# Down projection of a feed-forward block as seven block products in place of eight, in four parts shifted by one tile

## Chip, cores and metric

The kernel runs on one core of one Trainium2 chip. The metric is the device time of one execution in microseconds (us), the median of several runs. Five engines work side by side, each on its own queue in order: TensorE (PE; its weight loads are shown as PEld), VectorE (DVE), ScalarE (ACT), GpSimd (POOL), and SyncE (SP), which issues DMAs. POOL issues the accumulating DMAs.

## What is computed

One layer of a streaming encoder over 512 prompt tokens and 64 sample tokens (576 columns in all), model width 1024: a mixer with two linear-attention branches, a cross attention into 256 memory tokens, a feed-forward with a short convolution, and a last norm. The change lies in the feed-forward:

```python
def _conv_ffn(h, w_up, conv_w, conv_b, w_down, prev):
    u, new = _causal_dwconv(h @ w_up, conv_w, prev)      # width 3, along the tokens
    u = u + conv_b
    gate, val = u[..., :D_FF], u[..., D_FF:]             # D_FF = 2816 = 22 blocks of 128
    return (jax.nn.silu(gate) * val) @ w_down, new
...
x = x + f.astype(x.dtype)
...
y = _rmsnorm(x, p['norm_final'])
```

All of it is in fp32.

## The kernel before

**Layout.** Activations lie transposed: features on the 128 partitions, the 576 tokens along the free axis. A weight tile is 128 output features by up to eight blocks of 128 input features. An fp32 product is three matmuls on rounded operands (fp32r): each operand is split into a high part and a rest, and high x high, high x rest (activation's rest) and rest x high (weight's rest) are summed in PSUM. Names: `xh`/`xl` and `ach`/`acl` are high and rest of activations, `wh`/`wl` of weights, `wr` the raw weight from HBM.

**Weights.** `emit_weight` loads a raw tile (three raw buffers, `RAWB`), and for up and down projection makes the rest in three steps: ACT writes minus the raw weight, rounded, into `wl`; ACT casts the raw weight into `wh`; an accumulating DMA, issued by POOL, adds the raw weight to `wl`. For other weights, VectorE or POOL subtracts (`X` takes the one that the planner expects to be done first). `weight` hands out a tile and prepares one tile ahead (`LA`).

**Order.** The order on every engine is written by a planner in the kernel (`Driver`): TensorE's matmuls are taken in program order, and each instruction of another engine is put where the planner's own costs say that its engine is free, at most 6 us (`BACK`) before TensorE's planned time. Side work runs in generators (`spawn`) which go on when their inputs are planned to be ready. The chip then runs each queue in that order; semaphores do the rest.

**Feed-forward.** Two halves of 11 blocks. In each half, for each block, `tile_proj("up", ...)` runs the gate tile and the value tile (8 blocks x 3 terms x 2 column ranges = 48 matmuls each), and `up_finish` takes them out of PSUM with the norm's factor (`fu`), runs the three-step convolution (`fc`, one scaled copy and two multiply-adds on VectorE), then SiLU on ACT, the product of gate and value, and the split into `ach` and `acl`. Then the down projection of that half: for each of the eight output tiles, the 11 blocks go into one two-bank PSUM tile (`big`), in column ranges of 256 and 322 (two columns of padding between prompt and sample included), and VectorE adds the result to `x[m]`. With `late=True`, all matmuls with `wh` stand ahead of those with `wl`.

**End.** In the second half, each finished `x[m]` is squared (`sq`), summed (`acc`) and scaled with the last norm's gain (`gx`). The last output tile, 7, is computed in two column ranges (`half`), so that the norm and the transposes of the first (`c_out`, `rtf`, `yo`) run beside the matmuls of the second. PSUM has two `big` tiles and four single banks (`sm`).

Of the kernel before, what the change touches and what calls it, by code (L numbers as in the profile page):

```python
# [22 lines left out]
KT = D // P  # L23
EPS = 1e-6
NJ = 22
FH = 11
SLOT = 584
LA = 1
NS = 57
RAWB = 3  # L30
WB = 3
NGDN = 2
HOP = 0.2
BACK = 6.0
# [9 lines left out]
C_CB = 224  # L44
# [17 lines left out]
def weight_order():  # L62
    seq = list(HEADS)
    for m in range(8):
        seq += [("gta", m), ("gtb", m)]
    seq += [("out", m) for m in range(8)]
    seq += [("wo", m) for m in range(8)]
    for hd in range(4):
        seq += [("mk", 2 * hd), ("mk", 2 * hd + 1)]
        if hd % 2 == 0:  # L70
            seq += [("mv", 2 * hd + i) for i in range(4)]
        seq += [("mq", 2 * hd), ("mq", 2 * hd + 1)]
    seq += [("mo", m) for m in range(8)]
    for f in range(2):
        for j in range(FH * f, FH * f + FH):
            seq += [("up", j), ("up", NJ + j)]
        for m in range(8):
            seq += [("dn", (m, f, 0)), ("dn", (m, f, 1))]
    return seq


WORDER = weight_order()
WFULL = [w for w in WORDER if w[0] != "dn"]
WIDX = {w: i for i, w in enumerate(WFULL)}
NW = len(WFULL)

# [4 lines left out]
WAIT = "wait"  # L91
# [267 lines left out]
def tile_trunk(ctx, tc, xT, memT, wt, wd, vec, cst, w0, wgate, st_gdn, st_conv, st_gla, st_ffn, ckT, cv,  # L359
# [30 lines left out]
    def big():  # L390
        return drv.rotate("big", 2, pb.tile([P, 2, 512], F32, tag="big", name=nm("big")))
# [7 lines left out]
    def f(ap):  # L399
        return ap.bitcast(F32)  # L400
# [2 lines left out]
    wpos = [0]  # L403
    wready = {}

    def emit_weight(i):
        kind, idx = WORDER[i]
        raw = drv.rotate("raw", RAWB, wp.tile([P, 1024], F32, tag="raw", name=nm("wr"), bufs=RAWB))
        if kind == "dn":
            m, fh, part = idx  # L410
            n = (6 if part == 0 else 5) * 128
            c0 = fh * FH * 128 + part * 768
            DMA(raw[:, :n], wd[m, :, c0:c0 + n])
        else:
            n = 1024
            DMA(raw, wt[WIDX[(kind, idx)]])
        h = drv.rotate("wh", WB, wp.tile([P, 1024], F32R, tag="wh", name=nm("wh"), bufs=WB))
        lo = drv.rotate("wl", WB, wp.tile([P, 1024], F32R, tag="wl", name=nm("wl"), bufs=WB))
        if kind in SUMMED:
            A.activation(lo[:, :n], raw[:, :n], AF.Copy, scale=-1.0)  # L420
            A.copy(h[:, :n], raw[:, :n])
            drv.accumulate(lo[:, :n], raw[:, :n], nc.gpsimd)
# [5 lines left out]
    def weight(kind, idx, ahead=LA):  # L428
        i = wpos[0]
        assert WORDER[i] == (kind, idx), (WORDER[i], kind, idx)  # L430
        wpos[0] = i + 1
        for j in range(i, min(i + ahead + 1, len(WORDER))):
            if j not in wready:
                emit_weight(j)
        return wready[i]


    ones_r = cp.tile([P, 128], F32R, name="onesr")
# [30 lines left out]
    def vcol(c, n=1):  # L469
        return vec_t[:, c:c + n]  # L470
# [53 lines left out]
    def two(t_, o1=0, o2=TP):  # L524
        return r4(t_[:, o1:o1 + TP], 256), t_[:, o2:o2 + TS]
# [692 lines left out]
    def main():  # L1218
        acc = slot("acc")
        xg = []  # L1220
        for i in range(2):
            wready[i] = tuple(wp.tile([P, 1024], F32R, tag=t_, name=nm(t_), bufs=WB) for t_ in ("wh", "wl"))
            drv.rotate("wh", WB, wready[i][0])
            drv.rotate("wl", WB, wready[i][1])
        acc2 = slot("acc")
        s1 = slot("sq")

# [244 lines left out]

        drv.spawn(c_rstat("n3", [(acc, 0)], 4, True, 2.0))
        CW = 578

        def up_finish(col, ps):
# [5 lines left out]
            G.tensor_copy(fout[:, col, 2:4], u[:, 578:580])  # L1482
            c = slot("fc")
# [6 lines left out]
        for fh in range(2):  # L1490
            act = []
            for j in range(FH * fh, FH * fh + FH):
# [6 lines left out]
                c0 = up_finish(j, ba_[0])  # L1499
                A.activation(c0[:, 0:CW], c0[:, 0:CW], AF.Silu)  # L1500
                if j > 0:
                    yield from tile_proj("up", NJ + j, xs, bb_)
                c1 = up_finish(NJ + j, bb_[0])
                X.tensor_tensor(c0[:, 0:CW], c0[:, 0:CW], c1[:, 0:CW], op=ALU.mult)
                h, lo = slot("ach", F32R), slot("acl", F32R)
                A.copy(h[:, 0:CW], c0[:, 0:CW])
                X.tensor_tensor(lo[:, 0:CW], c0[:, 0:CW], f(h[:, 0:CW]), op=ALU.subtract)
                act.append((h[:, 0:CW], lo[:, 0:CW]))
            if fh == 0:
                for m in range(8):  # L1510
                    ps = big()
                    wh, wl = weight("dn", (m, fh, 0))
                    yield from proj(ps, wh, wl, act[0:6], True, False, CW, late=True)
                    wh, wl = weight("dn", (m, fh, 1))
                    yield from proj(ps, wh, wl, act[6:11], False, True, CW, late=True)
                    xx = two(x[m])
                    V.tensor_tensor(xx[0], xx[0], ps[:, :, 0:256], op=ALU.add)
                    V.tensor_tensor(xx[1], xx[1], ps[:, 1, 258:322], op=ALU.add)
            else:
                DMO(o_ffn, fout)  # L1520

        acc = slot("acc")
        gx = []
        for m in range(7):
            ps = big()
            wh, wl = weight("dn", (m, 1, 0))
            yield from proj(ps, wh, wl, act[0:6], True, False, CW, late=True)
            wh, wl = weight("dn", (m, 1, 1))
            yield from proj(ps, wh, wl, act[6:11], False, True, CW, late=True)
            xx = two(x[m])  # L1530
            V.tensor_tensor(xx[0], xx[0], ps[:, :, 0:256], op=ALU.add)
            V.tensor_tensor(xx[1], xx[1], ps[:, 1, 258:322], op=ALU.add)
            sq_acc(acc, x[m], m == 0)
            g = slot("gx")
            A.activation(g[:, 0:T], x[m][:, 0:T], AF.Identity, scale=vcol(C_GFIN + m))
            gx.append(g)
        m = 7
        wa, wb = weight("dn", (m, 1, 0)), weight("dn", (m, 1, 1))
        sq7, g7 = slot("sq"), slot("gx")
        gx.append(g7)  # L1540

# [42 lines left out]
                    yield 0.0  # L1584

        def half(o, c):
            k = 0
            for (wh, wl), n in ((wa, 6), (wb, 5)):
                for i in range(n):
                    mm3([(o, c)], wh, wl, act[k][0], act[k][1], i, k == 0, k == 10)  # L1590
                    k += 1
                    yield 1.0

        halves = [sm(), big()[:, 0, :]]
        yield from half(halves[0][:, 0:322], slice(256, CW))
        last_evac(halves[0], (256, TP, 0), (TP, T, 258))
# [51 lines left out]
def pack_inputs(inp):  # L1648
# [26 lines left out]
    wd = np.stack([kp(a["w_down"][0][:, P * m:P * m + P]) for m in range(8)])  # L1675

    w0 = np.zeros((D, 32), np.float32)
    w0[:, 0:16] = w_in[:, off["glr"]:off["glr"] + 16]
# [62 lines left out]
```

## Time and profile before

| | |
|---|---|
| median of 3 runs | 1157.0 us (1156.87 to 1157.26) |
| the profiled execution | 1155.68 us, span of its instructions 1153.8 us |
| TensorE busy | 1131.2 us (98%), granted clock 0.996 on average |
| VectorE, ACT, POOL busy | 639.0 (55%), 476.3 (41%), 287.3 us (25%) |
| moved by DMA | 133.66 MB, 116 GB/s on average |

Busy time of TensorE is a modelled figure, since matmuls overlap; the chain of waits and the distance between the starts of matmuls say more. The program's lines nearly all show as one helper line (L179 before), so tiles' names tell the instructions apart: `big<-xh,wh` is an up projection (and others ahead of it), `big<-ach,wh` a down projection, `x<-x,big` its addition to the residual, `wl<-wr` on ACT the negation and on POOL the issue of the accumulating DMA. In groups of instructions the figures are count | busy us, mean ns of one | idle time of the engine ahead of them and what ended it.

### The profile page before, as it was taken

Reading aid. Unit: us, or ns where it says so; the run is one execution under the profiler, and the core shown is the slowest. Engines: PE = TensorE matmul, PEld = TensorE weight load, DVE = VectorE, ACT = ScalarE, POOL = GpSimd, SP = SyncE. Lnnn points to the kernel's source line nnn. Section 1 sums busy time; section 2 is a strip of 40 time slices with the busy share of each in tenths; the row PEclk is TensorE's granted clock in tenths of the full one; section 3 lists DMA queues with packets and bytes.
Section 4 is the critical chain, followed back from the end, with each engine's and each line's share of the span. In section 5 each row is a group of like instructions: output and inputs, shape, how many; then the busy total and the mean of one; then the engine's idle time right before and its main releaser. Section 6 shows DMA issues by size and latency. Waiting matters only on the chain.

```text
span 1153.8 us, 20892 instructions
## 1 busy us (share of the span) xinstructions
PE 1131.2 (98%) x8573; PEld 1092.4 (95%) x8573; DVE 639.0 (55%) x1122; ACT 476.3 (41%) x900; POOL 287.3 (25%) x470
## 2 busy tenths in 40 slices
PE   8989999999999999999999999999999999999998
PEld 7889899989889999999999999999999999999998
DVE  7798557687454347656565554566561036566213
ACT  5445336335443243234444343533433333443443
POOL 4473127533112011002021100322221122222211
PEclk9999999999999999999999999999999999999999
DMA  6131101211213233434334314577667877677773
GB/s 233 37 91 41 47 15 57 77 39 42 70 31 128 76 110 102 143 97 135 110 124 141 129 55 109 131 167 175 169 139 171 170 174 173 162 163 156 163 165 116
DMA packets 46862, 133.66 MB, mean 116 GB/s; under 512 B 5424, under 2 KB 10800, under 8 KB 46768
## 3 DMA queue, kind: packets, MB, share of 16 engines
q1 hardware_dynamic: 35824, 97.74, 26.8%
q0 software_dynamic: 10944, 34.61, 16.9%
q8 instruction: 67, 1.10, 0.4%
q14 instruction: 27, 0.22, 0.1%
HBM read 92.35 MB, written 5.37 MB: 85 GB/s over the span
## 4 chain that ended last, share of the span: by engine, by line
PE 89%; DVE 7%; ACT 1%; issue 1%; DMA 1%; SPq 0%; POOL 0%; ACTq 0%; DVEq 0%
PE big L179 76%; PE sm L179 13%; DVE c L179 3%; DMA x<-xT 1%; DVE acc L179 0%; DVE xl L179 0%; SPq L179 0%; ACT c L179 0%; DVE u L179 0%; DVE gc L179 0%; DVE tg L179 0%; DVE z L179 0%; DMA wr<-wt 0%; DVE gy L179 0%; ACT th L179 0%
## 5 line engine op out<-in xcount | busy, mean ns | idle before, releaser
L179 PE MATMUL big<-xh,wh 128*128 128x256 f32 (+1 forms) x1536 | 339.1, 302 | 2.6 <-DVE sg L179 1.8
L179 PE MATMUL big<-xl,wh 128*128 128x256 f32 (+1 forms) x1536 | 328.5, 295 | 1.8 <-DVE xl L179 1.8
L179 PE MATMUL big<-xh,wl 128*128 128x256 f32 (+1 forms) x1536 | 280.1, 296 | 1.5 <-DVE wl L179 1.3
L179 PEld LDWEIGHTS big<-xh,wh 128*128 128x128 f32 x1536 | 254.0, 189 | 7.4 <-issue 2.1
L179 PEld LDWEIGHTS big<-xl,wh 128*128 128x128 f32 x1536 | 258.1, 189 | 2.7 <-DVE xl L179 2.7
L179 PEld LDWEIGHTS big<-xh,wl 128*128 128x128 f32 x1536 | 237.6, 189 | 2.0 <-DVE wl L179 1.5
L179 ACT CAST wh<-wr 128x1024 fp32r<-128x1024 f32 (+3 forms) x170 | 166.5, 980 | 35.3 <-PE big L179 16.6
L179 POOL TENSOR_TENSOR wl<-wr,wh 128x1024 fp32r<-128x1024 f32 x37 | 91.8, 2480 | 265.3 <-ACT wh L179 238.3
L179 POOL DMA_DIRECT2D wl<-wr x76 | 66.3, 949 | 151.6 <-ACT wl L179 150.0
L179 ACT ACTIVATE wl<-wr 128x1024 fp32r<-128x1024 f32 (+1 forms) x76 | 71.6, 942 | 63.8 <-PE big L179 61.1
L179 DVE TENSOR_TENSOR fu<-big,rbc 128x512 f32<-128x512 f32 (+1 forms) x88 | 36.3, 454 | 88.3 <-PE big L179 85.4
L179 DVE TENSOR_TENSOR wl<-wr,wh 128x1024 fp32r<-128x1024 f32 (+1 forms) x57 | 69.4, 1218 | 24.8 <-ACT wh L179 24.4
L179 PE MATMUL big<-ach,wh 128*128 128x256 f32 x341 | 74.1, 296 | 0.0
L179 DVE SCALAR_TENSOR_TENSOR fc<-fu,vec,fc 128x578 f32<-128x578 f32 x88 | 72.3, 822 | 3.1
L179 PE MATMUL big<-acl,wh 128*128 128x256 f32 x341 | 74.0, 296 | 0.0
L179 DVE TENSOR_TENSOR x<-x,big 128x512 f32<-128x512 f32 (+2 forms) x32 | 12.8, 441 | 103.6 <-PE big L179 103.6
L179 POOL COPY fout<-fu 128x2 f32<-128x2 f32 x88 | 15.1, 199 | 189.1 <-DVE fu L179 189.1
L179 ACT ACTIVATE fc<-fc 128x578 f32<-128x578 f32 x22 | 15.2, 690 | 104.1 <-DVE fc L179 104.1
L179 PEld LDWEIGHTS big<-acl,wh 128*128 128x128 f32 x341 | 57.9, 189 | 0.0
L179 PEld LDWEIGHTS big<-ach,wh 128*128 128x128 f32 x341 | 57.7, 189 | 0.0
L179 DVE SCALAR_TENSOR_TENSOR c<-u,vec,c 128x579 f32<-128x579 f32 x36 | 49.6, 1383 | 5.0 <-ACT c L179 4.2
L179 PE MATMUL big<-ach,wl 128*128 128x256 f32 x341 | 52.1, 296 | 0.0
(327 smaller groups left out, 1893.4 us busy)
## 6 DMA issues: line engine op xcount, KB each, us to landing
wr<-wt SPq DMA_DIRECT2D x134, 512.0 KB, 3.9
wl<-wr POOLq DMA_DIRECT2D x44, 512.0 KB, 5.1
wr<-wd SPq DMA_DIRECT2D x16, 384.0 KB, 3.6
wl<-wr POOLq DMA_DIRECT2D x16, 384.0 KB, 4.4
wr<-wd SPq DMA_DIRECT2D x16, 320.0 KB, 3.5
wl<-wr POOLq DMA_DIRECT2D x16, 320.0 KB, 4.7
x<-xT SPq DMA_DIRECT2D x16, 288.0 KB, 4.1
o_y<-yo SPq DMA_DIRECT2D x8, 256.0 KB, 2.4
```

Of the source, the lines that this page charges most:

```text
L179: fn(*args, **kw)
```

## The change

The 22 blocks of the down projection are cut into four parts of 6, 6, 6 and 4. The products of a part stand one block's two up tiles after the part's last activation. In parts 0 to 2, all eight output tiles, taken in pairs, are computed by seven products in place of eight; in part 3 the tiles 2 to 5 are, and tiles 0, 1, 6 and 7 stay plain.

For a pair of output tiles (m, m+1), the even and the odd blocks of a part and the two halves of the tokens (`N1`, `N2`, 288 columns each) make 2 x 2 blocks: weights a11, a12 (tile m, even and odd), a21, a22 (tile m+1); activations ce and co, each with halves 1 and 2. The products are P1 = a11 ce1, P2 = a12 co1, Q5 = (a21+a22) u1, Q6 = (a21+a22+a11) w1, P3 = (a21+a22+a11+a12) co2, Q7 = (a11+a21) u2, Q4 = a22 w2, with u1 = ce1-ce2, u2 = co2-ce2, w1 = -u2-ce1, w2 = -w1-co1 (`operands`, on VectorE). P1, Q6, Q7 and Q4 add up in one PSUM bank, Q5 and P3 in a second, P2 has a third; after each product, VectorE adds the bank to, or takes it from, one half of x[m] or x[m+1]. So a bank is written again only after its last evacuation. The order is P1, Q5, Q4 of the pair before, Q6, P2, P3, Q7.

Weight sums are made on VectorE (`ws`), cast on ACT, and their rests subtracted on VectorE or POOL; P1, P2 and Q4 use single weights and the accumulating DMA as before. A product's weights are one tile of 1024 columns (high parts in the first half, rests in the second), from a ring of six which takes the place of the three `wh` and three `wl`. `fetch` prepares five products, or two plain tiles, ahead. A pair holds two of the three raw buffers.

Beside that: the first step of the convolution moves from VectorE to ACT; convolution, SiLU and product become spawned generators; the padding columns are left out after the product (the product of gate and value is two instructions, 512 and 64 columns); the last output tile has 4 blocks left in place of 11.

```diff
-FH = 11
-LA = 1
+HT = T // 2
-WB = 3
+WB = 6
...
+PARTS = [list(range(0, 6)), list(range(6, 12)), list(range(12, 18)), list(range(18, 22))]
+PARTK = [p[0::2] + p[1::2] for p in PARTS]
+PART0 = [0, 6, 12, 18]
+
+def product_order(pairs):
+    seq = []
+    for i, pair in enumerate(pairs):
+        seq += [(pair, "P1"), (pair, "Q5")]
+        if i:
+            seq.append((pairs[i - 1], "Q4"))
+        seq += [(pair, p) for p in ("Q6", "P2", "P3", "Q7")]
+    return seq + [(pairs[-1], "Q4")]
+
+def ffn_order():
+    seq, late = [], []
+    for p, js in enumerate(PARTS):
+        for j in js:
+            seq.append(("up", j))
+            seq += late
+            late = []
+        late = [("dns", [(m, p) for m in range(0, 8, 2)])]
+    return seq + [("dn", (0, 1)), ("dns", [(2, 3), (4, 3)]), ("dn", (6, 7))]
...
+    def split_summed(h, lo, raw):
+        A.activation(lo, raw, AF.Copy, scale=-1.0)
+        A.copy(h, raw)
+        drv.accumulate(lo, raw, nc.gpsimd)
+
+    def emit_product(pair, prod):
+        m, p = pair
+        n = len(PARTS[p]) * 64
+        if prod == "P1":
+            r = halves_of[pair] = []
+            for i in range(2):
+                raw = raw_tile()
+                DMA(raw[:, :2 * n], wd[m + i, :, PART0[p] * 128:PART0[p] * 128 + 2 * n])
+                r += [raw[:, 0:n], raw[:, n:2 * n]]
+        r = halves_of[pair]
+        a11, a12, a21, a22 = r[:4]
+        def total(a, b):
+            s_ = slot("ws")
+            V.tensor_tensor(s_[:, 0:n], a, b, op=ALU.add)
+            r.append(s_[:, 0:n])
+            return s_[:, 0:n]
+        src = {"P1": lambda: a11, "Q5": lambda: total(a21, a22), "Q6": lambda: total(r[4], a11), "P3": lambda: total(r[5], a12),
+               "Q7": lambda: total(a11, a21), "P2": lambda: a12, "Q4": lambda: a22}[prod]()
+        w = w_tile()
+        h, lo = w[:, 0:n], w[:, 512:512 + n]
+        if prod in ("P1", "P2", "Q4"):
+            split_summed(h, lo, src)
+        else:
+            A.copy(h, src)
+            X.tensor_tensor(lo, src, f(h), op=ALU.subtract)
+        return h, lo
...
+    def fetch(i, room):
+        for j in range(i, len(WORDER)):
+            room -= 1 if WORDER[j][0] == "dn*" else 2
+            if room < 0:
+                break
             if j not in wready:
                 emit_weight(j)
...
+        def up_conv(col, u):
             c = slot("fc")
             w = C_CW + 3 * col
-            V.tensor_scalar(c[:, 0:CW], u[:, 0:CW], vcol(w), vcol(C_CB + col), op0=ALU.mult, op1=ALU.add)
+            A.activation(c[:, 0:CW], u[:, 0:CW], AF.Identity, scale=vcol(w), bias=vcol(C_CB + col))
             for i in range(1, 3):
+                yield [c]
                 V.scalar_tensor_tensor(c[:, 0:CW], u[:, i:i + CW], vcol(w + i), c[:, 0:CW], op0=ALU.mult, op1=ALU.add)
...
+        def operands(ke, ko, ce, co, whole):
+            u, w = slot("tu"), slot("tw")
+            V.tensor_tensor(u[:, N2], co[:, N2], ce[:, N2], op=ALU.subtract)
+            yield [u]
+            V.tensor_tensor(u[:, N1], ce[:, N1], ce[:, N2], op=ALU.subtract)
+            yield [u]
+            V.scalar_tensor_tensor(w[:, N1], u[:, N2], -1.0, ce[:, N1], op0=ALU.mult, op1=ALU.subtract)
+            yield [w]
+            V.scalar_tensor_tensor(w[:, N2], w[:, N1], -1.0, co[:, N1], op0=ALU.mult, op1=ALU.subtract)
+            fu = hl2(u)
+            yield [fu[1]]
+            fw = hl2(w)
...
+        def products(pairs):
+            banks = {}
+            for pair, prod in product_order(pairs):
+                m, p = pair
+                kes = PARTS[p][0::2]
+                n = len(kes)
+                bank = pair, "b" if prod in ("Q5", "P3") else "c" if prod == "P2" else "a"
+                start = bank not in banks
+                if start:
+                    banks[bank] = sm()
+                o = banks[bank][:, 0:HT]
+                wh, wl = weight("dn*", (pair, prod))
+                for i, ke in enumerate(kes):
+                    h, lo = ops[ke][prod]
+                    PE.matmul(o, wh[:, 128 * i:128 * i + 128], h, start=start and i == 0, stop=False, skip_group_check=True)
+                    PE.matmul(o, wh[:, 128 * i:128 * i + 128], lo, start=False, stop=False, skip_group_check=True)
+                    yield 0.4
+                for i, ke in enumerate(kes):
+                    PE.matmul(o, wl[:, 128 * i:128 * i + 128], ops[ke][prod][0], start=False, stop=i == n - 1, skip_group_check=True)
+                xx, op = (x[m], ALU.add) if prod in ("P1", "Q6", "P3", "P2") else (x[m + 1], ALU.subtract)
+                half = N1 if prod in ("P1", "P2", "Q4") else N2
+                V.tensor_tensor(xx[:, half], xx[:, half], o, op=op)
+                fetch(wpos[0], 5)
+                yield 0.4
```

More of the change, by code (lines that the diff above doesn't have):

```diff
@@ L1221, in main @@
         for i in range(2):
[L1222 to L1224 removed]
+            wready[i] = (w_tile(), w_tile())
         acc2 = slot("acc")
@@ L1507, in main @@
[L1507 to L1510, printed above, removed]
-                    ps = big()
[L1512 to L1536, printed above, removed]
+                drv.spawn(c_act(j, up_evac(NJ + j, bb_[0])), 1)
@@ new lines, in main @@
+                if j == NJ - 1:
+                    DMO(o_ffn, fout)
+            elif kd == "dns":
+                yield tuple(("act", j) for j in PARTS[i[0][1]])
+                yield from products(i)
+            else:
+                yield tuple(("act", j) for j in PARTS[3][:-1])
+                halves = []
+                for m in i:
+                    ps = big()
+                    wh, wl = weight("dn", (m, 3), m == i[0])
+                    yield from proj(ps, wh, wl, [full[k] for k in PARTK[3][:-1]], True, False, late=True)
+                    halves.append((ps, wh, wl))
+                yield (("act", NJ - 1),)
+                for m, (ps, wh, wl) in zip(i, halves):
+                    yield from proj(ps, wh, wl, [full[NJ - 1]], False, True, k0=len(PARTS[3]) - 1)
+                    for xx, i_ in zip(two(x[m]), pv(ps)):
+                        V.tensor_tensor(xx, xx, i_, op=ALU.add)
+                    last_tile(m)
@@ L1537, in main @@
+        act = act_of(3)
+        m = 6
+        ps = big()
+        wh, wl = weight("dn", (m, 3))
+        yield from proj(ps, wh, wl, act, late=True)
+        for xx, i_ in zip(two(x[m]), pv(ps)):
+            V.tensor_tensor(xx, xx, i_, op=ALU.add)
+        last_tile(m)
         m = 7
-        wa, wb = weight("dn", (m, 1, 0)), weight("dn", (m, 1, 1))
+        wa = weight("dn", (m, 3))
         sq7, g7 = slot("sq"), slot("gx")
```

139 lines of the change are left out of this document (100 added, 39 removed).

## The prediction

> **What bounds the kernel now.** I read the page first (span, engines, chain), then the chain in order of time, then the engines' busy time by stage, and last the start times of single matmuls. On the chain, the columns are start, length and what ran.
>
> ```profile
> PE 1131.2 (98%) x8573; PEld 1092.4 (95%) x8573; DVE 639.0 (55%) x1122; ACT 476.3 (41%) x900; POOL 287.3 (25%) x470
> PE 89%; DVE 7%; ACT 1%; issue 1%; DMA 1%; SPq 0%; POOL 0%; ACTq 0%; DVEq 0%
> 732.16 400.87 PE big L179 x3026
> ```
>
> TensorE (PE) carries 89% of the chain, and from 732 us to 1133 us, nearly the whole feed-forward, it never waits. So there a matmul taken away is time taken away, until something else comes late. The stages (window in us; its length and PE busy; then PEld, DVE, ACT, POOL) show how much room the others have:
>
> ```profile
> 735.00:876.00 141.00, 141.00 (x1071) 141.00 (x1070) 82.18 (x130) 57.98 (x70) 34.46 (x103) 1.00 0.70 161
> 861.00:932.00 71.00, 71.00 (x534) 71.00 (x533) 10.31 (x21) 25.17 (x33) 14.35 (x21) 1.00 0.80 170
> 1133.00:1153.80 20.80, 15.40 (x127) 15.06 (x125) 7.80 (x20) 5.76 (x11) 2.31 (x4) 0.94 0.33 115
> ```
>
> Row one is up projection: VectorE (DVE) 58% busy. Row two is the first down projection: DVE 15%, ACT 35%. Row three is the tail. The granted clock (the 1.00) is full.
>
> The profiled execution took 1155.7 us with a span of 1153.8; the median of the runs is 1157.0. I sum differences against the trace and take them off 1157.0. A measurement tells some 0.2%, 2.3 us, from no change.
>
> Ahead of the feed-forward, each engine's instructions stand in the same order and shape in both kernels (the weight buffers change names only), so the first 720 us are put at no change.
>
> **Matmuls: the gain.** The pace is the distance between starts:
>
> ```profile
> 741.18 0.43 PE L179 MATMUL big<-xh,wh 128*128 128x256 f32 x2
> 747.51 0.43 PE L179 MATMUL big<-xh,wh 128*128 128x256 f32 x2
> 875.01 0.43 PE L179 MATMUL big<-ach,wh 128*128 128x256 f32 x2
> 879.03 0.43 PE L179 MATMUL big<-ach,wh 128*128 128x256 f32 x2
> ```
>
> Between the first two starts stand one up tile's 48 matmuls, half 256 and half 320 columns wide: 6.33/48 = 0.1319 us each, at 288 columns on average. Between the last two stand 30 down matmuls (256 and 322): 4.02/30 = 0.134 us. Down projection now has 8 tiles x 22 blocks x 3 terms x 2 halves = 1056 matmuls: 141.5 us. After, parts 0 to 2 have 4 pairs x 7 products x 3 blocks x 3 terms = 252 each, part 3 has 84 for its two pairs and 96 for its four plain tiles: 756 + 84 + 96 = 936, all of 288 columns on average: 936 x 0.1319 = 123.5 us. **Gain 18.0 us**, all on the path by the 400.87 us row.
>
> The Trainium skill (TensorE: Matmul & The Clock Gate, Back-to-back issue gap) puts a warm matmul alone at N/2.4 + 2.5 ns: 122.5 ns at 288 columns. By it the gain would be, as an estimate, 15.1 us and the time 3 us later; the trace's 0.1319 us disagrees, and I keep the rows.
>
> **VectorE in the three long product stages: the main cost.** The instruction order puts this between the first and last evacuation of such a stage: 28 evacuations of 288 columns (two per plain tile before), 27 operations of 384 columns (sums of weights and low halves; only two or so low halves go to POOL), two convolution steps of the next up tile.
>
> ```profile
> L179 DVE TENSOR_TENSOR x<-x,big 128x512 f32<-128x512 f32 x15 | 10.3, 688 | 102.7 <-PE big L179 102.7
> L179 DVE TENSOR_TENSOR ba<-sm,rbc 128x320 f32<-128x320 f32 x1 | 0.5, 481 | 0.0
> L179 DVE TENSOR_TENSOR x<-x,sm 128x256 f32<-128x256 f32 x1 | 0.4, 422 | 2.5 <-PE sm L179 2.5
> L179 DVE TENSOR_TENSOR acl<-fc,ach 128x578 fp32r<-128x578 f32 x22 | 16.8, 762 | 16.0 <-ACT ach L179 16.0
> L179 DVE SCALAR_TENSOR_TENSOR fc<-fu,vec,fc 128x578 f32<-128x578 f32 x88 | 72.3, 822 | 3.1
> ```
>
> By these, 288 columns take 0.45 us, 384 take 0.55, a step 0.82: 12.6 + 14.9 + 1.6 = 29.1 us. TensorE needs 27 products x 9 matmuls x 0.1319 = 32.1 us meanwhile. So DVE goes from 15% to 91%. To that come waits: a low half follows its cast on ACT, and the acl row shows 16.0/21 = 0.76 us of idling per such step. In the new order at least one evacuation (0.45) stands between sum and low half nearly always, leaving 0.3 us, some 13 times: 29.1 + 4.0 = 33.1 us against 32.1. Bounds: no cost (five products are prepared ahead, and a PSUM bank is written again one to three products later, 1.2 to 3.6 us) and 0.76 x 13 - 3 = 7 us per stage. I take **1 us each, 3 in all**, nearest to the sum.
>
> The Trainium skill (VectorE: DVE Perf Modes, the TRN2 errata section) speaks against this change: a fixed latency is paid per instruction, so use tiles of 512 or more. The rows agree: 256 columns cost 0.42 us and 512 cost 0.69, so 0.15 of each op is fixed; it stands in the sum already.
>
> **Last product stage** (two pairs, 256-column weights): 14 evacuations x 0.45 + 12 weight operations x 0.42 + two accumulations x 0.76 = 12.9 us of DVE against 13 products x 6 x 0.1319 = 10.3 us of PE. **2.6 us lost**; bounds 0 (it is worked off ahead and behind) and 5 (ACT has the squares and gains of finished tiles among its casts).
>
> **The last activation.** Now, from the end of the up matmuls:
>
> ```profile
> 1071.34 0.82 DVE L179 TENSOR_TENSOR fu<-big,rbc 128x512 f32<-128x512 f32 x2 [3.10 <-PE big L179]
> 1076.23 0.76 DVE L179 TENSOR_TENSOR acl<-fc,ach 128x578 fp32r<-128x578 f32 x1 [0.80 <-ACT ach L179]
> L179 ACT ACTIVATE c<-u,vec 128x579 f32<-128x579 f32 x12 | 9.3, 779 | 10.3 <-DVE u L179 8.4 <-POOL u L179 1.9
> ```
>
> 5.65 us, covered today by the matmuls of the ten earlier blocks. After, the convolution's first step is on ACT (0.78, not 0.58, and two hand-offs of 0.08) and two small DVE operations stand ahead of the low half: 5.9 us, 6.4 with a weight cast in ACT's way. Cover: two tiles x 3 blocks x 6 x 0.1319 = 4.75 us. **1.4 us lost** (1.1 to 1.7). At the three other ends of parts the cover is a whole up tile of two projections, 12.7 us, for this chain plus some 4 us of operand differences: nothing. In the up stages DVE gains 0.58 x 2 (to ACT) per block and pays 4 x 0.45 + 2 x 0.76 per two blocks for operands: still under 70%, nothing.
>
> **Weights.** Lead of the first up tile after products: three products, 3.6 us, plus the up to 6 us by which the planner may put work ahead (BACK).
>
> ```profile
> L179 ACT ACTIVATE wl<-wr 128x1024 fp32r<-128x1024 f32 x44 | 46.3, 1052 | 18.8 <-PE big L179 16.4 <-DMA wr<-wt 2.4
> L179 ACT ACTIVATE wl<-wr 128x640 fp32r<-128x640 f32 x16 | 11.8, 738 | 25.9 <-PE big L179 25.5 <-DMA wr<-wd 0.4
> L179 POOL DMA_DIRECT2D wl<-wr x17 | 14.7, 862 | 57.4 <-ACT wl L179 57.1 <-issue 0.3
> wr<-wt SPq DMA_DIRECT2D x134, 512.0 KB, 3.9
> wl<-wr POOLq DMA_DIRECT2D x44, 512.0 KB, 5.1
> wr<-wd SPq DMA_DIRECT2D x16, 384.0 KB, 3.6
> wl<-wr POOLq DMA_DIRECT2D x16, 384.0 KB, 4.4
> ```
>
> Load 3.9 + two casts 2.1 + accumulate 5.1 = 11.1 us, against 9.6 + 4.2 (the low half is used after 32 matmuls). It fits, with less room than one whole tile gives now. On SP's queue the next pair's second load waits for a raw buffer (three exist, a pair holds two); behind it wait the loads of the next pairs, and TensorE after them: 3.6 + sum 0.55 + cast 0.5 + low half 0.55 + hand-offs = 5.5 us against five products, 5.9, plus what is put ahead. Bounds 0 and 1 us at each of 14 pairs; at the three seams and the last plain tiles I take 0.5 each: **1.9 us**.
>
> **Tail.** The last tile's halves have 12 matmuls each in place of 33.
>
> ```profile
> 1132.87 0.31 PE L179 MATMUL sm<-ach,wh 128*128 128x322 f32 x1
> 1139.93 0.28 PE L179 MATMUL sm<-cst,acc 128*128 128x1 f32 x2
> 1144.05 0.36 PE L179 MATMUL big<-ach,wh 128*128 128x256 f32 x1
> 1145.78 0.28 PE L179 MATMUL big<-ach,wl 128*128 128x256 f32 x1
> ```
>
> Today the 4.1 us of sums and transposes for the first half (1139.93 to 1144.05) stand inside the second half's matmuls, and from its last matmul to the end are 8.0 us. After, the halves take 3.2 us; if the 4.1 us all go behind them, the tail is 3.2 + 4.1 + 8.0 = 15.3 us, exactly what the gain above counts; if all run beside the norm's other steps, 11.2. But the first half's chain of square, sum, power and scaling loses its cover. I take 14.3: **1 us gained** (bounds -4.1 and +2).
>
> **Sum:** -18.0 + 3 + 2.6 + 1.4 + 1.9 - 1.0 = -10.1 us: 1157.0 - 10 = **1147.0 us** (a profiled execution of about 1145.6).
>
> **Rivals.** *VectorE becomes the bound (slower).* If every low half finds its cast late by the full 0.76 us (for: the acl row; casts share ACT with the next up tile's), a pair costs DVE 7 x 0.45 + 8 x 0.55 + 4 x 0.76 = 10.6 us against TensorE's 8.3: +2.3 for each of 12 pairs, 27.6 us in place of my 3, so about 1171. It decides from 9.4 us a pair on, where the gain is used up. Against: the evacuations that stand between. Chance 0.13. *Weights come late at every pair (no change or slightly slower):* +1 us at 14 pairs in place of 1.9: about 1159; at two thirds of that, 1154. Against: the work put ahead. 0.09. *POOL's queue comes late.* The accumulating DMAs' issue took 0.86 us in the first down stage beside a quiet DVE; a DVE subtraction beside POOL arithmetic shows what shared access can do:
>
> ```profile
> L179 DVE TENSOR_TENSOR kvl<-kraw,kvh 128x512 fp32r<-128x512 f32 x4 | 9.4, 2341 | 2.9 <-ACT kvh L179 2.9
> ```
>
> 2.34 us against 0.69 for as many columns, 3.4 times. Were the 12 issues of a stage stretched so, 35 us of POOL in 32, then 3 us per stage: about 1156, no change. Against: hardly any POOL arithmetic is left in these stages. 0.03. The Trainium skill (GPSIMD Engine Reference, Key points) states such contention with two-input DVE instructions. *The change does not do what it says* is excluded: the matmuls counted above stand in the built program.
>
> **How the numbers follow.** The forecast has 0.75; its own range, with costs between nothing and twice what I took, is 1138 to 1156. The range 1140 to 1161 adds the late weights and the beginning of the VectorE case, and leaves out about 0.1 above (its far part) and 0.08 below. Faster by over 0.2%: 0.76 (the forecast, and the mildest late weights); within 0.2%: 0.06; slower: 0.18 (VectorE 0.13, the rest of the late weights).
>
> **What would show it.** Right: 120 matmuls fewer on TensorE, 288-wide ones 0.132 us apart; in the product stages DVE about 90% busy and TensorE without a wait over 1 us; a gap of 1 to 2 us before the last activation's matmuls. Wrong: pairs over 8.3 us apart; matmuls of P1 or Q5 that wait for a load or an accumulating DMA; evacuations that start over 1.2 us after their product; a longer tail than 15.3 us.

## The result: 1171.9 us, slower, and the profile after

The changed kernel takes 1171.9 us (median of 4 runs, 1171.68 to 1172.6), the kernel before 1157.1 on the same chip: ratio 1.0129, interval 1.0111 to 1.0147. The forecast was 1147.0. The profiled execution has a span of 1169.9 us, 16.1 more than before, and the feed-forward (from the start of its long run of up matmuls, at 732.1 us before and 732.7 after, to the end) went from 421.7 to 437.2 us.

The page of the changed kernel, busy time and the chain by engine:

```profile
PE 1128.3 (96%) x8453; PEld 1081.6 (92%) x8453; DVE 725.1 (62%) x1316; ACT 540.4 (46%) x1050; POOL 338.1 (29%) x520
PE 78%; DVE 10%; DMA 5%; issue 3%; ACT 3%; POOL 0%; SPq 0%; ACTq 0%; DVEq 0%; POOLq 0%
```

The 120 matmuls are gone (8573 to 8453), but TensorE has fallen from 89% to 78% of the chain. DMA has 4 points of the 11 that it lost (of its 5%, accumulating DMAs of weights are 2.8% and raw loads for the down projection 1.9%), VectorE 3, ACT and issue 2 each. The stages of the changed kernel (window; length, PE, PEld, DVE, ACT, POOL busy, granted clock, DMA share, GB/s): three long product stages, the last product stage, the tail.

```profile
811.40:850.90 39.50, 35.12 (x255) 33.77 (x254) 28.26 (x58) 19.72 (x40) 13.45 (x19) 1.00 0.63 137
927.30:968.70 41.40, 35.52 (x254) 33.71 (x253) 28.09 (x62) 19.39 (x39) 11.80 (x15) 1.00 0.62 137
1044.70:1084.30 39.60, 36.66 (x255) 35.24 (x254) 28.78 (x62) 19.88 (x40) 11.83 (x15) 0.96 0.62 142
1129.80:1149.00 19.20, 13.77 (x87) 12.19 (x86) 15.44 (x36) 14.22 (x30) 7.46 (x8) 0.95 0.44 85
1152.80:1169.90 17.10, 11.88 (x86) 11.27 (x84) 7.68 (x20) 5.86 (x11) 2.35 (x4) 0.83 0.39 139
```

A long stage has 252 matmuls, 33.2 us at 0.1319; the three take 120.5, so 20.8 us are lost there, where 3 (and some of 1.9) were forecast. VectorE is busy for 28 us of 40: it is not full. So something stops it. The waits (engine and tile, what it waited for: us in total, times, longest), first of all engines from 800 to 1150 us, then of PE:

```profile
DVE ws L211 <- DMA wr<-wd: 19.4, 11, 3.1
...
PE sm L211 <- DVE x L211: 8.5, 8, 2.3
PE sm L211 <- DMA w<-wr: 6.9, 5, 2.0
PE sm L211 <- ACT w L211: 2.7, 4, 1.1
```

VectorE's weight sums (`ws`) wait 19.4 us for raw weights, 11 times, ten of them for the 12 pairs of the long stages. TensorE's own waits in the long stages are 6.9 us for weights that an accumulating DMA completes, 3.4 us for evacuations and 2.5 us for casts; the other 5.1 us behind `x` lie in the last part. One place in the chain where a sum waits (start, length, what ran):

```profile
825.72 0.56 DVE ws L211
826.35 3.51 DMA wr<-wd
829.88 0.57 DVE ws L211
830.55 0.52 ACT w L211
831.14 0.44 issue
831.57 0.45 DVE x L211
```

and in the timeline (start, length, engine; last, in brackets, idle time and what ended it):

```profile
826.35 2.92 SPq L211 DMA_DIRECT2D wr<-wd  x2
829.88 0.56 DVE L211 TENSOR_TENSOR ws<-wr 128x384 f32<-128x384 f32 x1 [2.42 <-DMA wr<-wd]
830.36 0.45 DVE L211 TENSOR_TENSOR x<-x,sm 128x288 f32<-128x288 f32 x1
831.12 0.40 PE L211 MATMUL sm<-ach,w 128*128 128x288 f32 x1 [1.10 <-ACT w L211]
```

Read from above: the last reader of a raw buffer, a pair's Q7 sum, ends at 826.3; only then does SP issue the next pair's load. It lands 3.5 us later. VectorE has stood still for 2.42 us with the next sum at the head of its queue. Two things wait with it: the sum's cast, for which TensorE's next product stands still for 1.10 us here, and the evacuations behind the sum (830.36, 831.57), on which TensorE spends 0.33 us more at 832.91.

The accumulating DMA reads a raw buffer too, and can be the reader that the load waits for, as here, 8 us earlier in the same chain:

```profile
813.83 4.56 DMA w<-wr
818.44 3.03 DMA wr<-wd
```

### The profile page after: what moved, and what is told of

Its sections match the earlier page's. It is cut to its first block, busy times and chain, and to the rows that moved or that the text cites. A ratio compares the mean times of both kernels' runs of the same rounds, so it can differ in the third digit from the quotient of the medians.

```text
span 1169.9 us, 21282 instructions
## 1 busy us (share of the span) xinstructions
PE 1128.3 (96%) x8453; PEld 1081.6 (92%) x8453; DVE 725.1 (62%) x1316; ACT 540.4 (46%) x1050; POOL 338.1 (29%) x520
## 4 chain that ended last, share of the span: by engine, by line
PE 78%; DVE 10%; DMA 5%; issue 3%; ACT 3%; POOL 0%; SPq 0%; ACTq 0%; DVEq 0%; POOLq 0%
PE big L211 62%; PE sm L211 16%; DVE c L211 3%; DMA w<-wr 3%; DMA wr<-wd 2%; ACT w L211 1%; DVE x L211 1%; DVE w L211 1%; DVE ws L211 1%; DVE acc L211 1%; DMA x<-xT 1%; DVE fc L211 0%; DVE xl L211 0%; SPq L211 0%; ACT c L211 0%
## 5 line engine op out<-in xcount | busy, mean ns | idle before, releaser
L211 PE MATMUL big<-xh,w 128*128 128x256 f32 (+1 forms) x3072 | 563.1, 299 | 3.3 <-DVE sg L211 1.8
L211 PEld LDWEIGHTS big<-xh,w 128*128 128x128 f32 x3072 | 467.7, 189 | 9.0 <-issue 2.6
L211 PE MATMUL big<-xl,w 128*128 128x256 f32 (+1 forms) x1536 | 328.8, 296 | 2.3 <-DVE xl L211 2.2
L211 PEld LDWEIGHTS big<-xl,w 128*128 128x128 f32 x1536 | 258.5, 189 | 3.1 <-DVE xl L211 3.1
L211 ACT CAST w<-wr 128x1024 fp32r<-128x1024 f32 (+3 forms) x184 | 164.6, 897 | 32.1 <-PE big L211 15.2
L211 POOL TENSOR_TENSOR w<-wr,w 128x1024 fp32r<-128x1024 f32 x37 | 92.0, 2486 | 264.2 <-ACT w L211 241.1
L211 PE MATMUL sm<-ach,w 128*128 128x288 f32 (+1 forms) x496 | 108.4, 305 | 13.7 <-DVE x L211 8.5
L211 POOL DMA_DIRECT2D w<-wr x90 | 78.4, 878 | 146.3 <-ACT w L211 126.5
L211 PEld LDWEIGHTS sm<-ach,w 128*128 128x128 f32 x496 | 83.3, 192 | 18.9 <-DVE x L211 6.7
L211 ACT ACTIVATE w<-wr 128x1024 fp32r<-128x1024 f32 (+3 forms) x90 | 69.9, 776 | 17.8 <-DMA wr<-wt 10.2
L211 ACT ACTIVATE fc<-fu,vec 128x578 f32<-128x578 f32 x44 | 38.4, 873 | 66.7 <-DVE fu L211 65.1
L211 DVE TENSOR_TENSOR x<-x,sm 128x288 f32<-128x288 f32 (+1 forms) x100 | 42.8, 444 | 12.3 <-PE sm L211 12.2
```

Of the source, the lines that this page charges most:

```text
L211: fn(*args, **kw)
```

## The experiments

Three theories at first. **A**: the three raw buffers hold back the next pair's load, and VectorE's in-order queue waits behind each late sum. **B**: VectorE has too much to do in the product stages. **C**: GpSimd's arithmetic slows VectorE. Times of the kernel before, on the chip of each batch, were 1155.35 us (first four runs), 1156.75 (fourth raw buffer; last part plain), 1155.34 (55 slots; no sums with the fourth buffer), 1157.47 (no sums, low halves on VectorE) and 1156.35 (the two in a new order).

**A ring of four.** Two general slots fewer make room:

```diff
-NS = 57
-RAWB = 3
+NS = 55
+RAWB = 4
```

> A fourth raw weight buffer (and two of the 57 general buffers fewer, to make room; TensorE's, SyncE's order stays the same, a few instructions of ACT and POOL move). Theory A, the raw ring: a pair of output tiles holds two of three raw buffers, so on SyncE's queue the second load of the next pair waits for the last weight sum of this one (Q7's, on VectorE), and the load (3.1 to 3.6 us), its sum and its cast then stand in the open, with VectorE's and ACT's queues in order behind them. A: the three long product stages go from 39.5, 41.4, 39.6 us to about 35, the last from 19 to 16: about 1156 in all. Theory B, VectorE's own work is the bound: no change, 1170 to 1173. Theory C, arithmetic on POOL slows VectorE down: no change.

Measured: 1163.6 us, ratio 1.0068 (1.0052 to 1.0084). The long stages fell from 39.5, 41.4 and 39.6 us to 35.5, 34.2 and 34.4. The last product stage took 18.2 us, where 16 was expected, and the 733 us ahead of the long run of up matmuls became 8 us longer, so this run alone leaves two edits mixed.

**X always VectorE in the feed-forward.**

```diff
-            best = min(self.engines, key=lambda e: e.when([(name, args, kw)]))
+            best = self.engines[0] if self.engines[0].drv.ffn else min(self.engines, key=lambda e: e.when([(name, args, kw)]))
...
```

> In the feed-forward, VectorE alone does what the planner otherwise divides between VectorE and POOL (products of gate and value, low halves, sums of squares); POOL keeps its small copies and the issue of DMAs. Theory C (a VectorE operation beside arithmetic on POOL takes up to three times as long; 1.58 us in place of 0.55 was seen in the first product stage, and TensorE waited 1.6 us behind it): each product stage 2 to 3 us shorter, about 1164. Theory A (raw ring): 1170 to 1173. Theory B (VectorE's work is the bound): slower, about 1175.

Measured: 1169.7 us, ratio 1.0113 (1.0041 to 1.0184); the long stages took 38.7, 38.7 and 39.9 us, 3.2 less in all, and the last up stage gave 2.0 back. So C costs about 1 us in each long stage of the profiled run, net of the work that VectorE takes over; the time itself, two runs 6 us apart, can't be told from that of the changed kernel. Where C strikes in the changed kernel's timeline:

```profile
820.44 1.90 POOL L211 TENSOR_TENSOR fc<-fc,fc 128x512 f32<-128x512 f32 x2 [3.52 <-DVE fc L211]
820.57 1.58 DVE L211 TENSOR_TENSOR ws<-ws,wr 128x384 f32<-128x384 f32 x1
```

A sum that takes 0.55 us alone takes 1.58 beside GpSimd's product.

**No weight sums.**

```diff
-            s_ = slot("ws")
-            V.tensor_tensor(s_[:, 0:n], a, b, op=ALU.add)
-            r.append(s_[:, 0:n])
-            return s_[:, 0:n]
+            r.append(a)
+            return a
```

> The sums of weights are left out: each product uses its first term alone. It leaves out 4 of the 8 VectorE operations on weights per pair (7 us per long stage). Theory B (VectorE's work is the bound): the long stages fall to 34 us, about 1153. Theory A (raw ring): the buffer is still held, until ACT has cast Q7's weight; only 0.55 us of sum and a hand-off leave the chain of each pair: 1 us per pair, about 1160. Theory C: no change of its own.

Measured: 1180.6 us, ratio 1.0207 (1.0151 to 1.0263), long stages 43.6, 42.1 and 42.8 us: less work on VectorE, and slower. That speaks against B, but no theory had said "slower"; four later runs were needed to understand it.

**All tiles plain, in four parts.** The staging without the seven products, and without the split of tiles 0 and 1 around the last activation:

```diff
-            seq += [("dn*", u) for u in product_order(i)]
+            seq += [("dn", u) for u in i]
...
```

> Four parts, shifted by one tile, with the convolution's first step on ACT and spawned generators, but every output tile of every part plain (eight block products, one weight tile each, split as before). 1056 down matmuls again. If the pairs are what costs (A, B or C): stages of 38.0 us for parts 0 to 2 without a wait of TensorE, and about 1158 to 1161 in all, with a wait of some 3 us at the last activation, which has no cover here. If the division in parts or the spawned convolution costs: waits in or behind the up stages, over 1165.

Measured: 1164.0 us, ratio 1.006 (1.0029 to 1.009). One of its long down stages:

```profile
925.50:963.50 38.00, 38.00 (x291) 38.00 (x289) 9.57 (x20) 16.03 (x19) 8.19 (x13) 1.00 0.88 186
```

288 matmuls in 38.0 us without a gap. The parts and their shift by one tile cost nothing at the three inner seams; this run lost its time in its last part, 7.8 us: one wait of 4.9 us for the last activation, and half the granted clock (0.50) from 1120.7 to 1127.5. And it is the yardstick: as whole tiles a part takes 38.0 us, as pairs in the changed kernel 39.5 to 41.4.

**A fourth raw buffer without other edits.** A tile that the feed-forward does not use holds every fourth row:

```diff
-                raw = raw_tile()
+                raw = csamp.rearrange("p a b -> p (a b)") if i and m in (0, 4) else raw_tile()
```

> One edit to the changed kernel: in the pairs of tiles (0,1) and (4,5) the second raw weight row is loaded into a tile that the feed-forward does not use otherwise, so that two pairs' rows can be held at once without a larger ring and without fewer slots (which the earlier run with a ring of four had to pay for). Theory A (the ring of three raw buffers holds back the loads, and VectorE's in-order queue waits behind each late sum): the three long product stages take 34.2 to 35.5 us each instead of 39.5 to 41.4, as in the run with a ring of four, the first 720 us stay as in the changed kernel, and the time is 1171.9 - 16 = 1156, between 1153 and 1159, which is about that of the kernel before. Theory B (VectorE's work) and theory C (GpSimd's arithmetic beside VectorE): the long stages stay at 38.7 to 41 us and the time at 1168 to 1172. If the gain of the ring of four was due to the smaller number of slots, nothing moves here: 1170 to 1173.

Measured: 1154.1 us (11 runs), ratio 0.9975 (0.9966 to 0.9984): 17.8 us less than the changed kernel, by one buffer. TensorE's order is the same. Its long stages, and a piece of its last product stage:

```profile
811.10:846.80 35.70, 34.27 (x255) 33.56 (x254) 28.43 (x58) 20.90 (x40) 14.27 (x20) 1.00 0.68 150
922.70:957.00 34.30, 33.75 (x255) 33.52 (x254) 28.35 (x62) 20.46 (x39) 13.04 (x18) 1.00 0.73 156
1032.90:1067.10 34.20, 33.66 (x254) 33.42 (x253) 28.40 (x62) 20.72 (x39) 14.03 (x18) 1.00 0.72 155
...
1110.00:1115.00 5.00, 3.71 (x24) 3.25 (x24) 4.89 (x9) 3.32 (x8) 2.40 (x3) 1.00 0.18 26
1115.00:1120.00 5.00, 3.26 (x18) 3.29 (x19) 4.85 (x14) 4.46 (x12) 1.83 (x4) 0.80 0.38 82
```

120.5 us became 104.2: **16.3 us were the raw ring**, 1.4 per pair. VectorE's busy time in the stages is the same 28.4 us as before, in 34 to 36 us in place of 40. TensorE's waits for weights in the long stages (9.4 us) are gone, and 2.4 us behind evacuations are left of 3.4. So theory A is shown for the ring. How much of the 16.3 us went through VectorE's queue this run does not separate; by these waits it was the smaller part. The last two rows are another matter: there VectorE is full. The chain at that place:

```profile
1109.71 0.46 DVE tu L211
1110.17 0.34 DVE ws L211
1110.51 0.67 DVE acl L211
1111.17 1.62 DVE tw L211
1112.82 0.47 DVE tw L211
1113.31 0.68 ACT ach L211
1114.02 0.76 DVE acl L211
1114.77 1.83 DVE x L211 x5
1116.74 8.95 PE sm L211 x54
```

The operand differences (`tu`, `tw`) and splits of the last activation stand on VectorE ahead of the evacuations of tiles 0 and 1 and of P1; TensorE stops for 2.5 us, from 1114.1 on, for a bank. The first `tw` took 1.6 us, 0.45 in the stages before; GpSimd was subtracting a low half beside it (1.42 us from 1111.05), so C has a part in this stop.

**The last part plain as well.** The pairs (2,3) and (4,5) of part 3 become whole tiles, and the operands of that part go:

```diff
-            seq += [("dn*", u) for u in product_order(i)]
+            seq += [("dn", u) for u in i] if i[0][1] == 3 else [("dn*", u) for u in product_order(i)]
...
-            if odd_:
+            if odd_ and p < 3:
...
```

> The same as the run with the fourth raw buffer, and the last part (four k-tiles) takes all eight of its tiles as whole tiles in place of two pairs by seven products; the operand sums of the last activation go, the split of the first two tiles around the last activation stays. Matmuls: 96 of 288 columns' pairs in place of 84 in four tiles, 12 x 0.132 = 1.6 us more. The last product stage lost 8.0 us against its matmuls in the changed kernel and 7.1 us with a ring of four. If these are the operand sums, casts and loads of the pairs of that stage (theory D), the stage's loss falls to 1 to 2 us: the time is that of the fourth raw buffer alone - 6 + 1.6, about 4 us below it, near 1152. If they come from the last tiles' squares and casts, which stay here (theory E), it is 0 to 2 us above that of the fourth raw buffer alone.

Measured: **1149.2 us** (6 runs), ratio 0.9932 (0.9918 to 0.9946), 4.8 below the run before it; span 1147.9 against 1150.6, with 12 matmuls more. The same two stretches:

```profile
1110.00:1115.00 5.00, 3.32 (x16) 2.78 (x17) 2.40 (x5) 3.54 (x7) 1.73 (x2) 0.84 0.41 84
1115.00:1120.00 5.00, 5.00 (x34) 5.00 (x33) 1.58 (x3) 2.95 (x6) 0.85 (x1) 0.82 0.80 143
```

VectorE's backlog is gone (4.0 us busy in these 10 in place of 9.7). From the first matmul of tile 0 to the last of tile 6 it takes 26.1 us for 168 matmuls, against 28.7 for 156. The loss fell from 8.1 us to 4.0, not to 1 or 2: the wait for the last activation takes 2 us, and about as much goes to a lower clock behind it (0.84 and 0.82). So theory D holds for half of it; operands, weight sums and loads went together here, and their shares are not told apart.

**55 slots, ring of three** (`NS = 55` alone).

> The changed kernel with 55 general slots in place of 57, the ring of raw buffers at three. The run with a ring of four and 55 slots spent 8 us more than the changed kernel in its first 740 us, behind one stop of TensorE of 3.3 us at 295. If that came from the slots: 1171.9 + 8 = about 1180 here, with the stop in the trace. If it came from the ring of four or from chance: 1170 to 1173. The long product stages stay at 39.5 to 41.4 us under theory A, since their raw ring is unchanged.

Measured: 1180.0 us, ratio 1.0207 (1.0189 to 1.0225), long stages 39.9, 40.5 and 39.1. TensorE's wait from 280 to 320 us, which the changed kernel doesn't have:

```profile
PE sm L211 <- DVE SB L211: 3.3, 1, 3.3
```

So the 8 us of the ring of four came from the slots, as the first reading said; the edit that seemed a free trade cost a stop in another stage.

**No sums, with the fourth raw buffer.**

> The fourth raw buffer together with the edit of the earlier run without sums: each of the four weight sums of a pair is left out and its first operand is used in its place, so the output of the feed-forward is another one; VectorE does 48 sums less, some 7 us less in each long product stage. Without the fourth buffer that edit made the kernel slower (1180.6 against 1171.9). Reading A' (it was slower because without the sum the raw buffer itself stays in use until the cast and the subtraction of Q7, so that the next load starts later; a ring matter again): with four buffers the long stages take 33.5 to 35.5 us and the time is that of the fourth raw buffer alone, 1154 within 2. Reading B' (the sums' VectorE time holds the long stages where the ring no longer does): the stages fall from 34.2 to the matmuls' 33.2 and the time is 3 to 4 us below, 1150 to 1151. If the edit itself costs something that has nothing to do with buffers, it is some 8 us slower here too, near 1162.

Measured: 1172.2 us, ratio 1.0133 (1.0109 to 1.0157), long stages 39.6, 39.6 and 42.3. Neither A' nor B'; the third case, and 10 us further than it expected. Its groups (count | busy us, mean ns | idle ahead) showed one thing that moved:

```profile
L211 POOL TENSOR_TENSOR w<-wr,w 128x384 fp32r<-128x384 f32 x13 | 14.9, 1171 | 7.9 <-ACT w L211 7.8
L211 POOL TENSOR_TENSOR w<-csamp,w 128x384 fp32r<-128x384 f32 x8 | 9.1, 1139 | 11.3 <-ACT w L211 11.3
```

Without sums the planner gives 21 of 46 low halves to GpSimd. The next two runs bind them to VectorE, with four raw buffers and with three:

```diff
-            X.tensor_tensor(lo, src, f(h), op=ALU.subtract)
+            V.tensor_tensor(lo, src, f(h), op=ALU.subtract)
```

> As the run without weight sums and with a fourth raw buffer (each sum replaced by its first operand, so the feed-forward's output is another one), but the low halves of the product weights are bound to VectorE. In the two runs without sums the planner had put 21 and 22 of the 46 low halves of the three long stages on GpSimd, 1.1 us each, in the queue that issues the accumulating DMAs; with the sums it put one there. Reading G (that move to GpSimd is what made them slow): the long stages fall from 39.6 to 42.3 us to between 33.3 and 34.5 and the time is 1150 to 1155. Reading W (the order on VectorE is at fault: evacuations behind subtractions that wait for a cast and a free weight tile): the stages stay at 38 us or more and the time at 1168 or more. Theory B (VectorE's work is what is left of the long stages' loss): G's case, with stages at 33.3 in place of 34.2.

> The same edit with the ring of three raw buffers, as in the changed kernel: without sums, low halves on VectorE. Theory A (the ring holds back the loads, whatever VectorE's work is): the long stages stay between 38 and 42 us, the time at 1167 to 1175, though VectorE does 7 us less per stage. If the ring costs only together with a busy VectorE, the stages fall to 34 to 36 us and the time to 1153 to 1160.

Measured: with four 1163.1 us, ratio 1.0041 (1.0028 to 1.0055), long stages 39.0, 38.9 and 38.5; with three 1179.3, ratio 1.0201 (1.0173 to 1.0229), stages 40.7, 41.9 and 43.3. The ring costs here too (A, third time), and more than expected: of the 16.2 us between the two runs 9.5 lie in the long stages and 5.1 in the last product stage. Reading G explains only a part: the time fell by 9 us, but the stages stayed at the 38 us or more that reading W expected. What is left, in the timeline of the run with four:

```profile
837.15 0.51 ACT L211 CAST w<-wr 128x384 fp32r<-128x384 f32 x1 [0.73 <-PE sm L211]
...
837.69 0.56 DVE L211 TENSOR_TENSOR w<-wr,w 128x384 fp32r<-128x384 f32 x1 [0.32 <-ACT w L211]
...
838.17 0.45 DVE L211 TENSOR_TENSOR x<-x,sm 128x288 f32<-128x288 f32 x1
...
838.76 0.37 PE L211 MATMUL sm<-ach,w 128*128 128x288 f32 x1 [0.51 <-DVE x L211]
```

ACT's cast waits until TensorE has left a weight tile, the subtraction waits for the cast, and an evacuation stands behind the subtraction; TensorE waits for that. The weights that hold VectorE up here are for a product further on. Reading W needs only another order:

```diff
-            A.copy(h, src)
+            A.together([("copy", (h, src), {})], 1.0)
```

> As the run without sums, low halves on VectorE and a fourth raw buffer (the feed-forward's output is another one), and one number more: the planner counts 1 us extra for ACT's cast of a product's weights, so that it puts the subtraction behind it later among VectorE's evacuations; no instruction is added. Reading W (the last 5 us of a long stage without sums come from evacuations that stand behind a subtraction which still waits for its cast and a free weight tile): the stages fall from 38.5 to 39.0 us to 34 to 36 and the time from 1163 to 1148 to 1154. If the order on VectorE does not matter, stages and time stay: 1161 to 1165.

Measured: 1150.6 us, ratio 0.9957 (0.9943 to 0.9972), long stages 34.5, 34.3 and 34.4; W is shown. The first stage of the run with four, no sums, and then the same stage in the new order:

```profile
812.50:851.50 39.00, 35.60 (x254) 33.75 (x254) 20.97 (x45) 21.67 (x40) 13.16 (x18) 1.00 0.64 137
```

```profile
808.50:842.90 34.40, 33.76 (x254) 33.56 (x253) 21.65 (x47) 20.80 (x40) 10.71 (x17) 1.00 0.71 149
```

Equal work on VectorE, 4.6 us apart. In this stage VectorE's waits for casts fell from 9.9 us to none, TensorE's for evacuations from 3.3 us to 0.6. And against the fourth buffer with all its sums: 28.4 us of VectorE's work or 21.6, the stage takes 34.2 to 34.4 either way. So theory B falls for the long stages. (Of this run's time, some 3 us against the changed kernel come from a shorter stretch ahead of the feed-forward, where nothing was edited.)

**The best version in that order too.** The same extra microsecond in the kernel with the last part plain:

> The best version so far (fourth raw buffer, last part plain, 1149.2) with the same extra microsecond in the planner's cost of the casts. With the sums there VectorE's order has evacuations between nearly all sums and subtractions already, and the long stages stand at 34.2 us with one stop of 0.7: reading W gives at most 0.7 us a stage, so 1147 to 1150. If the later subtractions make weights late, the stages get longer: 1152 or more.

Measured: 1152.5 us, ratio 0.9964 (0.9951 to 0.9977); long stages 35.9, 35.5 and 35.1, so the second of the two expectations. With the sums in, the order was better as it was. The best of all runs stays 1149.2 us.

## Why the prediction was wrong, step by step

- **Weights: the step that failed.** It put 1.9 us; the raw ring alone cost 16.3. The text had the mechanism ("the next pair's second load waits for a raw buffer") and priced the rival at up to 1 us a pair, 1159 us. It went wrong in two ways. It compared 5.5 us of preparation with a lead of five products, as if the load went out with the request; but the load goes out when the last reader of an old buffer is done, here at 826.35, and TensorE's need does not move that. And it charged the wait at the three seams and the last plain tiles alone (at 0.5 each, which makes 2.0 and not 1.9), while it came inside the stages, at nearly every pair. It came mostly as TensorE's waits for the weights themselves: 6.9 us for accumulating DMAs, which the text had named as a sign of being wrong, and 2.5 for casts. The text left out that a late sum also holds the finished products behind it in VectorE's queue, but in the long stages that was the smaller part (3.4 us, of which 2.4 stay with the fourth buffer). In the third of these stages 1.7 us more went to a half clock behind two stops (0.50 from 1065.1 to 1068.5). Chance 0.09 was too low for something that no row bounded.
- **VectorE in the long stages.** 1 us each was forecast. With the ring out of the way, 1.0 to 2.5 are left (34.2 to 35.7 against 33.2): the size was near. The reason was not: taking away 7 us of VectorE's work per stage changes nothing (34.4). The rival "VectorE becomes the bound" (91% busy) is refuted there; it was 83% in 34.2 us. Its time, about 1171, is the measured one by coincidence: low halves waited 7.5 us for their casts in the three stages together, not 0.76 us each. The count of VectorE's work, 29.1 us, was right (28.4). The row read as up projection runs into the down projection, which begins at 861.4; up to there VectorE was 61% busy, not 58%, and nothing hung on it.
- **Last product stage:** 2.6 forecast, 8.1 measured (19.2 less 84 x 0.1319 = 11.1). Here VectorE is the bound at the start (9.7 us of 10 with the fourth buffer): the step left out that the last activation's operands stand ahead of the evacuations. The text had set operands at nothing at the other seams, where "the cover is a whole up tile", and had no term for those of the last part.
- **Last activation:** 1.4 forecast, 1.25 measured (7.58 us for 48 matmuls). Right.
- **Matmuls:** 18.0 us. The pace was right. In the run with the fourth buffer, one piece of the chain is

```profile
922.90 32.25 PE sm L211 x243
```

that is 0.1327 us each against 0.1319: 0.2 us in a stage of 252, counted in the stages' losses here.
- **Tail:** 14.3 forecast, 17.1 measured, 16.9 with the fourth buffer and 16.7 with the last part plain. The first half's norm, sums and transposes now stand behind the matmuls, without cover, and at a clock of 0.83. What each of the two is worth no run separates.
- Sum of what was measured: -18.0 + 20.8 (long stages) + 8.1 + 1.25 + 1.8 for the tail (17.1 less 15.3) + 0.7 at tile 6 + 0.6 in the up stages + 0.6 ahead of the long run of up matmuls = 15.9, against 16.1 between the spans.

So the gain from the products is real: 38.0 us as plain tiles, 34.2 as fed pairs, 3.8 in each of the last two long stages, and 2.7 in the first (38.4 against 35.7). The change as made spent it on waiting for its own weights.

## What to carry to other kernels

Size a staging ring by how long its last reader holds a buffer plus the load's time, not by how far ahead requests are made; one more buffer was worth 17.8 us here, and the place to look for it was an unused tile. On an in-order engine, an operation that may wait for a load or a cast delays every evacuation behind it, so a half-busy engine can still set the pace: read what stands at the head of its queue, not its share. An experiment that "only takes work away" also moves what a planner decides; look at the new order before its time is read as a verdict on the work.

## What the runs showed of the hardware

A stop of 2.5 us was followed by half of TensorE's clock for a while. In the timeline with the fourth buffer:

```profile
1116.74 0.37 PE L211 MATMUL sm<-ach,w 128*128 128x288 f32 x1 [2.34 <-DVE x L211]
```

and in the stages (the clock is the third number from the end):

```profile
1114.55:1117.96 3.41, 1.22 (x9) 1.25 (x10) 3.41 (x10) 2.91 (x6) 1.62 (x2) 1.00 0.27 41
1117.96:1121.38 3.42, 3.42 (x16) 3.42 (x15) 3.12 (x9) 2.40 (x8) 1.73 (x2) 0.50 0.51 112
```

From 1118.05 to 1121.4 starts are 0.24 us apart in place of 0.13, 1.6 us in all. With the last part plain, the same followed a stop of 1.6 us (clock 0.84, then 0.82). The Trainium skill (TensorE: Matmul & The Clock Gate, HAM oscillation) tells of such half clocks after idle gaps of over some 3.4 us; these stops were shorter. So this stop cost 4.1 us in place of 2.5, which no term of the prediction's sum had.

Yet the length of a stop alone does not decide. The changed kernel stood still just as long, 2.5 us from 1131.4 on, and kept its clock:

```profile
1129.92:1133.34 3.42, 1.67 (x13) 1.43 (x11) 3.31 (x9) 2.31 (x6) 1.65 (x2) 1.00 0.00 0
1133.34:1136.75 3.41, 2.80 (x18) 2.46 (x18) 3.25 (x9) 3.41 (x9) 0.23 (x2) 1.00 0.55 115
```

In every trace the clock changes on a fixed grid of 3.41 us, the bounds of these four rows. This stop lay across two cells, so that TensorE was busy for 0.49 of the first; the stop before filled most of one cell, which left 0.36. From 720 us on, over all fourteen traces, each of the 28 cells at full clock with less than 0.44 of busy time was followed by one at half clock, three of the ten from 0.44 to 0.53, and none of the 57 from 0.53 to 0.80; four more, 0.81 busy, lie in the tails.

The Trainium skill (GPSIMD Engine Reference, Key points) says that GpSimd shares its SBUF interfaces with VectorE and contends with VectorE's instructions that have two SBUF inputs. The 1.58 us sum above, 0.55 alone, agrees. The run with X on VectorE won about 1 us in each long stage, net of the work that VectorE took over.
